# Layer 0 input of an MLA and Hyena trunk: adaLN weights loaded first, x divided by its rms ahead of adaLN, and the q projection moved among the filters with its result kept in DRAM

## The chip, the core and the metric

The kernel runs on one core of a Trainium2 chip. Matrix products run on TensorE (PE, whose weight loads the profile shows apart as PEld), elementwise work on VectorE (DVE) and ScalarE (ACT). Transfers are issued from two queues, that of SyncE (SP) and that of GpSimd (POOL), and carried out by the core's 16 DMA engines. The metric is the device time of one execution in microseconds (us), as the median of several runs; lower is better.

## What is computed

A trunk of two layers over 1024 latent tokens of width 1024, with 256 context tokens beside them. Layer 0 mixes tokens by multi-head latent attention (MLA), layer 1 by a Hyena long convolution. Each layer is x + gate * mixer(modulate(rmsnorm(x))), where shift, scale and gate come from a conditioning vector through adaLN. What matters here is the input side of layer 0, and the Hyena filters, which depend on weights alone and are worked out beside it. Cut from the reference, with the adaLN line and the line of the filters put in words:

```python
def rmsnorm(x, g):
    y = xf * lax.rsqrt(jnp.mean(xf * xf, axis=-1, keepdims=True) + NORM_EPS)
    return (y * g).astype(x.dtype)

def modulate(h, shift, scale):
    return h * (1 + scale) + shift
...
# adaLN: shift, scale, gate = split(silu(c) @ ada_w + ada_b)     a = modulate(rmsnorm(x, g), shift, scale)
cq, ckv, k_rope, gate = jnp.split(t @ w_in, splits, axis=-1)     # 384, 256, 64, 1024 columns
q = (rmsnorm(cq, q_norm_g) @ w_uq).reshape(B, n, MLA_HEADS, MLA_NOPE + MLA_ROPE)
kv = (rmsnorm(ckv, kv_norm_g) @ w_ukv).reshape(B, n, MLA_HEADS, MLA_NOPE + MLA_V)
...
# Hyena filters: an MLP over positions, times a decay, then transformed to the frequency domain
```

## The kernel before

Arrays lie transposed, features on the 128 partitions and tokens along the free axis, in tiles of 128x512 in fp32. A product whose operands carry more than one pass of TensorE keeps (`mm3`, L119 to L121) is made of three matmuls: each operand is split into a high and a low part (`split`: the ACT copy at L96 gives the high part, the DVE subtraction at L97 the low one), and high x high (L119), high x low (L120) and low x high (L121) are added in PSUM.

`layer0_in` (L446 to L626) covers everything up to attention. Its parts, by the names that the profile shows:

- **Weights.** `feed` and `weights` (L101 to L115) load pieces of the input projection (`wr`, 256 KB) and split them into `w`, two ahead of use. The list given to `feed` names the output blocks of 128 columns in their order of use: 0 to 7 are gates, 8 to 10 the latent kv and the rotary key, 11 to 13 the latent q.
- **adaLN** (`ada`, L147 to L177). For layer 0's shift and scale, 32 weight tiles `pg<-in_adaw` of 256 KB, four of them to each of eight groups of packed matmuls (`ad<-pg,sc`, L128). The rest of adaLN (32 tiles `aw<-in_adaw` of 512 KB in two buffers, groups `ad<-aw,sc`) is taken up beside the projections.
- **The rms** of x (`rms`, L360 to L393): squares on ACT, sums by packed matmuls with `ones` (L128), a transposition (L381) and a chain of small DVE instructions, L385 to L392, up to `rms`. `spread` (L395 to L401) broadcasts it over the partitions by transpositions into a PSUM tile R (L399).
- **`modulate`** (L403 to L408). For each tile x * gs * R on DVE (L406), the high part with the shift on ACT (L407), the low part on DVE (L408).
- **The filters** (`filters`, L271 to L361), a generator in eight groups g. In each, eight steps make `ph` (L318 and L319 on PE), multiply it by the decay `dec` (`kk`, L321 on DVE) and form sums and differences `kp` and `km` (L328, L329); then a transform (`rg`, `rt`, `blk`, L222 and L225 on DVE), the split of its blocks into `bh` and `bl`, and 75 matmuls `u<-bh,fm`, `u<-bl,fm` against transform tables `fm`, in blocks whose results `ko` are written to DRAM (`kd<-ko`, L351). The eight tables, 3.28 MB, come once, over POOL's queue (L295), after small POOL copies (L294) that wait for a tile given to the generator with `send`.
- **Projections** (`project`, `pj<-pg,w`). One output block is 48 matmuls of 128x512 over both token halves. `gates` passes it through SiLU and writes it to `gate_d` in DRAM. `latent_kv`, for x, and `context`, for the context tokens, norm their result (`normed`, L502 to L513, whose multiplication is L508), split it and write both parts to DRAM (`ckv_d`, `kr_d`). `latent_q` norms and splits directly into the SBUF tiles `cq` that attention reads.

The filters and the generator `work` (gates 0 to 5, `latent_kv`, `context`, the rest of adaLN) are interleaved: after every step of the filters, as many steps of `work` are taken as the ratio 60 to 120 allows (L604 to L609). When the filters are through, `attention_loads` (L629 to L651) loads kv and key back over POOL's queue (`ckv`, `krh`, `krl`), the attention weights are split, and meanwhile `latent_q` runs with gates 6 and 7 between its steps. The attention loop follows, whose first products are the keys (`pj<-ckv,wc`) and the queries (`pj<-cq,wb`, `pj<-cq,wa`).

Every engine runs its instructions in one fixed order that is written when the kernel is built. Buffers of the next stage are laid over those that the stage before releases, so that a load waits until their last reader or writer is done.

## Time and profile before

| | us |
|---|---|
| median of 3 runs | 1741.19 (1737.99 to 1742.52) |
| the profiled execution, its own time | 1735.72 |
| span of that execution in the profile | 1733.9 |
| first projection matmul of layer 0 | 78.09 |
| last filter matmul (`u`) | 407.34 |
| first product with the latent q | 440.91 |

The mean granted TensorE clock was 0.976 of full speed. In the rows of the profile, times count from the start of the span; a row of the timeline gives the start, the duration, engine, line, operation and tiles, and in brackets how long the engine was idle ahead of it and what released it. A row of instructions that follow one another is put together with its count (x8).

### The profile page before, as it was taken

What the parts mean: (1) busy time and instruction counts of PE and PEld (TensorE: products, weight loads), DVE (VectorE), ACT (ScalarE), POOL (GpSimd) and SP (SyncE); (2) the same over time, 40 slices, a digit from 0 to 9 for tenths busy, and PEclk for the clock granted to TensorE, in tenths of its full rate; (3) what the DMA queues carried; (4) which work ended last, traced back from release to release, by engine and by line L of the source; (5) the groups of instructions that cost most, each with busy time, mean ns of one, the idle gap of its engine ahead of it and who ended that gap; (6) DMA issues with size and microseconds to landing.
All of it is one profiled execution on the core that took longest, in us unless ns stands there. A gap on an engine that the chain in (4) does not pass through costs nothing.

```text
span 1733.9 us, 22766 instructions
## 1 busy us (share of the span) xinstructions
PE 1635.3 (94%) x8096; PEld 1300.2 (75%) x8096; DVE 1442.4 (83%) x2539; ACT 766.1 (44%) x1331; POOL 15.4 (1%) x43
## 2 busy tenths in 40 slices
PE   6799897898999999999999999999999999999995
PEld 2467676686788788788787777888888888887873
DVE  4885978895598899899889466999999999999856
ACT  4533444435455555455556345433433433433313
POOL 1000000000000000000000010000000000000000
PEclk8899998999999999999999999999999999999998
DMA  9777563436101001010013781332332332334555
GB/s 341 255 231 222 182 191 118 147 95 196 37 22 42 25 26 37 25 33 25 19 56 121 233 268 64 101 97 84 100 117 83 104 111 85 102 113 138 175 158 204
DMA packets 139030, 207.19 MB, mean 119 GB/s; under 512 B 13386, under 2 KB 67361, under 8 KB 138788
## 3 DMA queue, kind: packets, MB, share of 16 engines
q1 hardware_dynamic: 135780, 195.05, 35.7%
q0 software_dynamic: 3136, 10.69, 1.9%
q8 instruction: 64, 1.05, 0.2%
q14 instruction: 50, 0.41, 0.1%
HBM read 149.97 MB, written 53.61 MB: 117 GB/s over the span
## 4 chain that ended last, share of the span: by engine, by line
PE 79%; DMA 8%; DVE 8%; ACT 3%; issue 1%; SPq 1%; DVEq 0%; ACTq 0%
PE pj L121 13%; PE pj L119 13%; PE pj L120 12%; PE O L120 2%; PE S L119 2%; PE O L119 2%; PE S L811 2%; DMA kd<-ko 2%; PE O L121 2%; PE apx L747 2%; PE S L810 2%; PE S L121 2%; PE S L120 2%; PE apx L748 2%; DMA aw<-in_adaw 2%; PE fu L119 2%
## 5 line engine op out<-in xcount | busy, mean ns | idle before, releaser
L96 ACT CAST w<-wr 128x512 fp32r<-128x512 f32 (+1 forms) x154 | 93.7, 609 | 259.2 <-PE pj L120 134.3
L119 PE MATMUL pj<-a,w 128*128 128x512 f32 x512 | 203.3, 398 | 1.7 <-ACT a L407 1.6
L121 PE MATMUL pj<-a,w 128*128 128x512 f32 x512 | 203.3, 398 | 0.0
L120 PE MATMUL pj<-a,w 128*128 128x512 f32 x512 | 203.2, 397 | 0.0
L813 ACT ACTIVATE p<-S 128x512 f32<-128x512 f32 x160 | 95.5, 597 | 148.2 <-DVE acc L820 69.5
L97 DVE TENSOR_TENSOR w<-wr,w 128x512 fp32r<-128x512 f32 (+1 forms) x154 | 102.4, 673 | 56.5 <-ACT w L96 56.3
L96 ACT CAST bh<-raw 128x512 fp32r<-128x512 f32 x128 | 77.0, 620 | 88.8 <-DVE raw L1056 71.1
L119 PEld LDWEIGHTS pj<-a,w 128*128 128x128 f32 x512 | 96.5, 189 | 22.0 <-ACT a L407 2.4
L120 PEld LDWEIGHTS pj<-a,w 128*128 128x128 f32 x512 | 96.6, 189 | 19.8 <-DVE a L408 0.2
L121 PEld LDWEIGHTS pj<-a,w 128*128 128x128 f32 x512 | 96.7, 189 | 19.4 <-issue 0.8
L97 DVE TENSOR_TENSOR p<-p 128x512 fp32r<-128x512 f32 x160 | 109.5, 685 | 1.5 <-ACT p L96 1.2
L749 DVE TENSOR_REDUCE cm<-apx 128x1 f32<-128x512 f32 (+1 forms) x192 | 107.3, 592 | 3.8 <-PE apx L748 3.0
L121 PE MATMUL pj<-pg,w 128*128 128x512 f32 (+1 forms) x248 | 98.0, 395 | 9.5 <-DVE w L97 9.5
L820 DVE TENSOR_TENSOR acc<-acc,p 128x512 f32<-128x512 f32 x144 | 98.9, 687 | 7.6 <-ACT p L813 6.7
L96 ACT CAST p<-p 128x512 fp32r<-128x512 f32 x160 | 99.4, 622 | 4.8
L119 PE MATMUL pj<-pg,w 128*128 128x512 f32 (+1 forms) x248 | 96.7, 393 | 2.4 <-ACT pg L407 2.4
L120 PE MATMUL pj<-pg,w 128*128 128x512 f32 (+1 forms) x248 | 98.1, 396 | 0.6 <-DVE pg L408 0.6
L97 DVE TENSOR_TENSOR bl<-raw,bh 128x512 fp32r<-128x512 f32 x128 | 84.9, 688 | 9.1 <-ACT bh L96 8.9
L119 PE MATMUL u<-bh,fm 128*128 128x256 f32 (+1 forms) x200 | 67.8, 340 | 11.6 <-ACT bh L96 9.0
L321 DVE TENSOR_TENSOR kk<-ph,dec 128x512 f32<-128x512 f32 x64 | 42.9, 685 | 35.4 <-DMA dec<-in_dec 28.2
L747 PE MATMUL apx<-kn,qn 128*128 128x512 f32 (+1 forms) x192 | 69.1, 364 | 2.3 <-DVE cm L749 1.9
L748 PE MATMUL apx<-krh,r 128*128 128x512 f32 (+1 forms) x192 | 67.2, 358 | 0.0
(304 smaller groups left out, 4392.4 us busy)
## 6 DMA issues: line engine op xcount, KB each, us to landing
aw<-in_adaw SPq DMA_DIRECT2D x32, 512.0 KB
kd<-ko SPq DMA_DIRECT2D x128, 128.0 KB
wr<-in_hw SPq DMA_DIRECT2D x64, 256.0 KB
kt<-kd SPq DMA_DIRECT2D x56, 256.0 KB
wr<-in_w SPq DMA_DIRECT2D x34, 256.0 KB
dec<-in_dec SPq DMA_DIRECT2D x64, 128.0 KB
pg<-in_adaw SPq DMA_DIRECT2D x32, 256.0 KB
wr<-in_wo SPq DMA_DIRECT2D x32, 256.0 KB
```

The source lines that it names most:

```text
L96: self.nc.scalar.copy(out=hi, in_=raw)
L97: self.nc.vector.tensor_tensor(out=lo, in0=raw, in1=hi, op=ALU.subtract)
L119: mm(out, lhsT=w[0], rhs=x[0], start=start, stop=False)
L120: mm(out, lhsT=w[0], rhs=x[1], start=False, stop=False)
L121: mm(out, lhsT=w[1], rhs=x[0], start=False, stop=stop)
L321: nc.vector.tensor_tensor(out=kk, in0=ps, in1=dec.broadcast_to([P, 2, 2, P]), op=ALU.mult)
L747: mm(b[:, :w], lhsT=qn[0][:, c], rhs=kn[0][:, o : o + w], start=True, stop=False)
L748: mm(b[:, :w], lhsT=r1[:, c], rhs=krh[:, o : o + w], start=False, stop=True)
L749: v.tensor_reduce(out=cm[:, t, i : i + 1], in_=b[:, :w], axis=AX.X, op=ALU.max)
L810: mm(S, lhsT=krh[:, c], rhs=r1, start=False, stop=False)
L813: act.activation(out=p, in_=S, func=AF.Exp, scale=ASCALE)
L820: v.tensor_tensor(out=acc, in0=acc, in1=p, op=ALU.add)
```

## The change

The input of layer 0 is reordered and partly rewritten:

- `modulate` is replaced for layer 0 by two functions. `normalize` multiplies x by the spread rms in place (L415, DVE, one instruction for each tile). `shifted` then forms x * gs + shift twice, on ACT into the high part (L420) and on DVE in place (L421, TENSOR_SCALAR), and subtracts (L422, DVE). Layer 1 keeps `modulate`.
- The first half of x is normalised ahead of adaLN, its second half and the context later. The rms of the second half and of the context are worked out where they are used.
- The loop over adaLN's eight groups no longer steps the filters, so that nothing of them is asked for between the adaLN weights. The second half of x and the context are loaded behind these. The tables `fm` are released by the last tile of the second half of x (`x[1][7]`) rather than by that of the first.
- `latent_q` moves into `work`, behind `context`. Its result is written to DRAM (`cq_d`, six high and six low pieces of 256 KB) and loaded back by `attention_loads` with six loads of 512 KB on POOL's queue.
- Gates come in pairs, 0 and 1, 2 and 3, 4 and 5, and gates 6 and 7 last, behind the filters. The ratio of steps is now 66 to 128.

```diff
+    def normalize(self, xs, r, bank):
+        n = xs[0].shape[-1]
+        R = self.spread(r, n // P, bank)
+        for x in xs:
+            self.nc.vector.tensor_tensor(out=x, in0=x, in1=R[:, :n], op=ALU.mult)
+
+    def shifted(self, x, gs, sh, hi, lo):
+        nc = self.nc
+        nc.scalar.activation(out=hi, in_=x, func=AF.Identity, scale=gs, bias=sh)
+        nc.vector.tensor_scalar(out=x, in0=x, scalar1=gs, scalar2=sh, op0=ALU.mult, op1=ALU.add)
+        nc.vector.tensor_tensor(out=lo, in0=x, in1=hi, op=ALU.subtract)
...
+        self.cq_d = [self.dram.tile([KQ, P, L], F32, name=f"cq_d{r}") for r in range(2)]
...
-        self.feed([a["w1"][m] for m in (0, 1, 2, 8, 9, 10, 3, 4, 8, 9, 10, 5, 11, 12, 13, 6, 7)])
+        self.feed([a["w1"][m] for m in (0, 1, 8, 9, 10, 2, 3, 8, 9, 10, 11, 12, 13, 4, 5, 6, 7)])
...
         load_x(0)
-        rx = [self.rms(x[0], 512, bank, page)]
-        filt.send(x[0][7])
-        for n, _ in enumerate(self.ada([(0, 0, 4)], lambda n: page(), abank, 512)):
-            next(filt)
-            if n == 7:
-                load_x(1)
-                rx.append(self.rms(x[1], 512, bank, page))
+        self.normalize(x[0], self.rms(x[0], 512, bank, page), bank)
+        for _ in self.ada([(0, 0, 4)], lambda n: page(), abank, 512):
+            pass
+        load_x(1)
         load_c()
         xcs = [xc[k // 2][:, LC * (k % 2) : LC * (k % 2) + LC] for k in range(KD)]
-        rc = self.rms(xcs, LC, bank, page)
+        filt.send(x[1][7])
         ax = []
-        for xs, r in zip(x, rx):
-            R = self.spread(r, 4, bank)
+        for h, xs in enumerate(x):
+            if h:
+                self.normalize(xs, self.rms(xs, 512, bank, page), bank)
...
-                self.modulate(xs[k], R, gs[:, k, 0:1], res[:, k, 0:1], hi, lo)
+                self.shifted(xs[k], gs[:, k, 0:1], res[:, k, 0:1], hi, lo)
...
         def latent_q():
...
-            more = gates(range(6, 8))
             for h, sl in enumerate(halves):
-                for _ in normed([t[h] for t in ts], "qg", self.att[3], sl, True):
-                    next(more, None)
-                    yield
-            yield from more
+                yield from normed([t[h] for t in ts], "qg", self.cq_d, sl)
...
-            for _ in gates(range(0, 3)):
+            for _ in gates(range(0, 2)):
...
-            for _ in gates(range(3, 5)):
+            for _ in gates(range(2, 4)):
...
             yield from context()
-            for _ in gates(range(5, 6)):
+            yield from latent_q()
+            for _ in gates(range(4, 6)):
...
-            while n * 120 < (step + 1) * 60:
+            while n * 128 < (step + 1) * 66:
...
-        for _ in latent_q():
-            next(loads, None)
         for _ in loads:
             pass
+        for _ in gates(range(6, 8)):
+            pass
...
         nc.gpsimd.dma_start(out=krl, in_=self.kr_d[1])
         yield
+        for k in range(KQ):
+            for r in range(2):
+                nc.gpsimd.dma_start(out=cq[r][k], in_=self.cq_d[r][k])
```

What the change moves on PE ahead of the first projection. Before, filter matmuls `u` of the first group stand in front of `pj<-pg,w`; this is the end of that stretch:

```order
L119 MATMUL u<-bh,fm_103 128x256
L120 MATMUL u<-bl,fm_103 128x256
L121 MATMUL u<-bh,fm_104 128x256
L119 MATMUL u<-bh,fm_103 128x512
L120 MATMUL u<-bl,fm_103 128x512
L119 MATMUL pj<-pg,w 128x512
```

And now at the same place:

```order
L128 MATMUL ad<-aw,sc 32x512 x4
L128 MATMUL pj<-pg,ones 32x512 x4
L319 MATMUL ph<-fw,hr 128x256
L319 MATMUL ph<-fw,hf 128x256
L318 MATMUL ph<-fw,hr 128x256
L319 MATMUL ph<-fw,hr 128x256
L381 MATMUL pj<-ident,pg 128x128 x4
L128 MATMUL ad<-aw,sc 32x512 x4
L399 MATMUL pj<-ident,rms 128x128 x4
L119 MATMUL pj<-pg,w 128x512
```

No `u` stands ahead of the first projection any more (53 of them before, as counted over the whole order); five groups of the rest of adaLN (`ad<-aw,sc`, one before) and the sums, transposition and spread of the second half's rms do.

On SP's queue, before, from the first of the other adaLN weights (`aw`) to the second half of x, with the decay tiles `dec` between the adaLN weights:

```order
L156 DMA aw<-in_adaw 128x1024 x2
L156 DMA pg<-in_adaw 128x512 x8
L314 DMA dec<-in_dec 128x256
L156 DMA pg<-in_adaw 128x512 x4
L314 DMA dec<-in_dec 128x256
L156 DMA pg<-in_adaw 128x512 x4
L314 DMA dec<-in_dec 128x256
```

and now, at the same place:

```order
L156 DMA aw<-in_adaw 128x1024 x2
L156 DMA pg<-in_adaw 128x512 x32
L314 DMA dec<-in_dec 128x256 x2
L112 DMA wr<-in_w 128x512
L303 DMA fwr<-in_fwout 128x512
L112 DMA wr<-in_w 128x512
L481 DMA pg<-in_xT 128x512 x8
L485 DMA pg<-in_ctxT 128x512 x4
L156 DMA aw<-in_adaw 128x1024 x2
L314 DMA dec<-in_dec 128x256 x2
```

All 32 adaLN tiles stand back to back, and the last decay tiles of the first filter group stand behind x, the context and other adaLN weights.

On POOL's queue the loads for attention, before, were these seven:

```order
L641 DMA ckv_3997<-ckv_d_80 128x1280
L641 DMA ckv_3998<-ckv_d_80 128x1280
L641 DMA ckv_3999<-ckv_d_81 128x1280
L641 DMA ckv_4000<-ckv_d_81 128x1280
L646 DMA krh<-kr_d_82 64x1280 x2
L647 DMA krl<-kr_d_83 65x1280
```

and now, from the keys on (the four loads of `ckv` stand ahead of them as before):

```order
L654 DMA krh<-kr_d_84 64x1280 x2
L655 DMA krl<-kr_d_85 65x1280
L659 DMA cq_4332<-cq_d_82 128x1024
L659 DMA cq_4335<-cq_d_83 128x1024
L659 DMA cq_4333<-cq_d_82 128x1024
L659 DMA cq_4336<-cq_d_83 128x1024
L659 DMA cq_4334<-cq_d_82 128x1024
L659 DMA cq_4337<-cq_d_83 128x1024
```

Six loads of the latent q are new, last on the queue; the last of them (the third low piece) is first needed by the fifteenth matmul of the queries (before, by the eighth, since all of one weight's products stood ahead of the other's). Between the last `u` and the first query PE now has 37 projection matmuls and 18 of the keys; before it had 84 and 18, beside the norms of q.

More of the change, by code (lines that the diff above doesn't have):

```diff
@@ L500, in hilo_out, with normed @@
             nc.sync.dma_start(out=dsts[1], in_=lo.bitcast(F32)[:n])
-        def normed(xs, g, dst, sl, sbuf=False):
+        def normed(xs, g, dst, sl):
             n = sl.stop - sl.start
@@ L509, in normed @@
             for k, t in enumerate(xs):
-                if sbuf:
-                    self.split(t, dst[0][k][:, sl], dst[1][k][:, sl])
-                else:
-                    hilo_out(t, P, [d[k, :, sl] for d in dst])
+                hilo_out(t, P, [d[k, :, sl] for d in dst])
         def context():
-            R = self.spread(rc, 2, bank)
+            self.normalize(xcs, self.rms(xcs, LC, bank, page), bank)
+            yield
             ac = [[], []]
@@ L522, in context @@
                     sl = slice(LC * q, LC * q + LC)
-                    self.modulate(xcs[k + q], R[:, :LC], gs[:, k + q, 1:2], res[:, k + q, 1:2], hi[:, sl], lo[:, sl])
+                    self.shifted(xcs[k + q], gs[:, k + q, 1:2], res[:, k + q, 1:2], hi[:, sl], lo[:, sl])
                     ac[0].append(hi[:, sl])
```

## The prediction

> **What bounds the kernel now.** I read the page first, for the engine that sets the time, then the busy time by stretch, then PE's timeline in the stretches that the change touches.
>
> ```profile
> span 1733.9 us, 22766 instructions
> PE 1635.3 (94%) x8096; PEld 1300.2 (75%) x8096; DVE 1442.4 (83%) x2539; ACT 766.1 (44%) x1331; POOL 15.4 (1%) x43
> ```
>
> PE is busy for 94% of the span. A change in order can only gain where PE stands idle, and the change touches nothing behind the first queries of attention. So the question is how much PE idles up to there. The windows answer for it has, in each row, the stretch, its length, the busy time of the five engines, TensorE's clock, the DMA share and GB/s. The bounds are the first projection (78) and the last filter matmul with the start of the queries (407.5 and 440.9).
>
> ```profile
> 0.00:78.00 78.00, 52.99 (x252) 25.23 (x253) 47.76 (x112) 35.25 (x65) 5.76 (x20) 0.82 0.91 307
> 78.00:407.50 329.50, 296.68 (x1593) 234.94 (x1592) 270.46 (x558) 142.79 (x255) 0.00 (x0) 0.95 0.55 168
> 407.50:440.90 33.40, 27.75 (x122) 20.81 (x119) 13.46 (x25) 13.34 (x24) 3.69 (x7) 0.95 0.75 217
> ```
>
> PE idles 78.00 - 52.99 = 25.0 us in the start, where the DMA engines are busy for 0.91 of the time; 329.5 - 296.7 = 32.8 in the stretch of filters and projections, where DVE, at 270.5, is not far behind; and 33.4 - 27.75 = 5.7 in the tail. Those 63.5 us are all that can be had.
>
> **The change, part by part: the start.** PE's timeline shows what stood ahead of the first projection: adaLN's groups, waiting for weights, then the first filter matmul, then the first projection.
>
> ```profile
> 26.73 1.94 PE L128 MATMUL ad<-pg,sc 128*32 128x512 f32 x8
> 32.55 1.06 PE L128 MATMUL ad<-pg,sc 128*32 128x512 f32 x8 [1.90 <-DMA pg<-in_adaw]
> 52.34 1.94 PE L128 MATMUL ad<-pg,sc 128*32 128x512 f32 x8 [1.43 <-DMA pg<-in_adaw]
> 60.30 0.47 PE L119 MATMUL u<-bh,fm 128*128 128x512 f32 x1 [2.08 <-issue]
> 78.09 0.40 PE L119 MATMUL pj<-pg,w 128*128 128x512 f32 x1
> 79.73 1.07 PE L128 MATMUL ad<-aw,sc 128*32 128x512 f32 x8
> 85.77 1.07 PE L128 MATMUL ad<-aw,sc 128*32 128x512 f32 x8 [0.51 <-DMA aw<-in_adaw]
> 92.03 1.93 PE L128 MATMUL ad<-aw,sc 128*32 128x512 f32 x8 [1.47 <-DMA aw<-in_adaw]
> 101.15 1.06 PE L128 MATMUL ad<-aw,sc 128*32 128x512 f32 x8 [0.84 <-DMA aw<-in_adaw]
> ```
>
> adaLN now ends at 52.34 + 1.94 = 54.3. Its weights shared the DMA engines with the tables `fm`, which POOL issued as soon as the first half of x was there. The next rows are POOL's issue of them, and, from the DMA view of the first 60 us, the packets, MB and share of POOL's queue (q0) and the rate in 40 slices of 1.5 us.
>
> ```profile
> 13.68 4.39 POOL L295 DMA_DIRECT2D fm<-in_fm  x8
> q0 software_dynamic: 1152, 3.28, 15.2%
> GB/s 0 127 257 219 277 288 362 406 386 333 335 321 354 395 391 391 397 391 391 398 391 395 404 386 385 380 378 382 362 363 387 331 354 352 340 365 335 377 392 296
> ```
>
> Without the 3.28 MB of `fm` and the 128 KB decay tiles that stood between the weights, adaLN's last weight comes 3.28 / 0.39 = 8.4 us sooner for the tables, and some 4 to 5 for the rest: an estimate from these rows puts the last group at about 41, 13 us ahead. That is a gain only if the first projection follows. By the order it doesn't: between adaLN and the first projection PE now has five groups of the other adaLN weights instead of one. These come from two buffers and were 85.77 - 79.73 = 6.0 and 92.03 - 85.77 = 6.3 us apart. They stand on SP's queue behind the second half of x and the context (3.1 MB, 8 us at 391 GB/s). Five groups from about 41 + 8 on, 6 us apart, put the last at 49 + 4 x 6 = 73, beside the 3.28 MB of `fm`, which POOL now asks for at about 48 and which again run beside what PE waits for. On DVE, the second half's rms now stands behind the eighth product `kk`, whose decay tile comes behind those same weights, and behind the first transform. That transform took, before, from the end of this product to the first `u` at 60.30:
>
> ```profile
> 49.36 0.69 DVE L321 TENSOR_TENSOR kk<-ph,dec 128x512 f32<-128x512 f32 x1 [1.48 <-DMA dec<-in_dec]
> ```
>
> With that chain (11 us from the last `kk`, of which about half lies ahead of the rms) the first projection is possible at 72 to 84. I take 78, where it was: **0 us**, between -6 and +6.
>
> One rule of the Trainium skill speaks against loads on POOL's queue here. In the trace, the eight issues of `fm` took 4.39 us together, 0.55 each, with two instructions of the kind TENSOR_SCALAR on DVE in that time. The page "SBUF — State Buffer", in "SBUF: two separate sides", says that GpSimd can't write the descriptors of its transfers while a DVE instruction in a two-port mode holds the port pair that the two share. By that rule the eight new TENSOR_SCALAR (L421) of the first half, which run at about that time, would hold `fm` up by at most 8 x 0.44 = 3.5 us, by the durations below, and the sum would be 3.5 higher; the issues that the trace shows give no sign of such a delay, and I add nothing.
>
> **The stretch, PE.** Before, 84 projection matmuls of 128x512 stood behind the last `u`, those of q among them; now it is 37, of gates 6 and 7. The stretch gets the other 47. In a warm stretch one starts 435.25 - 435.02 = 0.23 us behind the other:
>
> ```profile
> 435.02 0.40 PE L121 MATMUL pj<-pg,w 128*128 128x512 f32 x1
> 435.25 0.39 PE L119 MATMUL pj<-pg,w 128*128 128x512 f32 x1
> 407.46 0.60 PE L399 MATMUL pj<-ident,rms 128*128 128x128 f32 x4
> 407.99 1.06 PE L128 MATMUL pj<-st,ones 128*32 128x512 f32 x6
> 410.01 0.50 PE L381 MATMUL pj<-ident,st 96*128 96x96 f32 x4
> 413.99 0.62 PE L399 MATMUL pj<-ident,rms 128*128 128x128 f32 x4 [0.48 <-DVE rms L392]
> ```
>
> That is 47 x 0.23 = 10.8, and the sums and spreads of q's norm, 0.60 + 1.06 + 0.50 + 0.62 = 2.8, come with it. The start gives up work as well: 53 of the first group's 75 matmuls `u` were done before 78.09 (14 of 512 columns at 0.23, 39 of 256 at half of it: 7.7) and the context's rms (about 1.5); none is done there now, while four more groups of `ad` (1.07 each, 4.3) are: +4.9. In all 10.8 + 2.8 + 4.9 = **18.5** of PE work more.
>
> **The stretch, DVE.** The rows by form, with count, sum and mean duration:
>
> ```profile
> L408 DVE SCALAR_TENSOR_TENSOR pg<-pg,adac 128x512 fp32r<-128x512 f32 x16 | 11.9, 745 | 3.6 <-ACT pg L407 3.6
> L406 DVE SCALAR_TENSOR_TENSOR pg<-pg,gs,pj 128x512 f32<-128x512 f32 x16 | 11.8, 741 | 0.0
> L508 DVE SCALAR_TENSOR_TENSOR pg<-pg,cols,pj 128x512 f32<-128x512 f32 x10 | 7.0, 744 | 4.1 <-PE pj L399 4.1
> L97 DVE TENSOR_TENSOR cq<-pg,cq 128x512 fp32r<-128x512 f32 x6 | 3.9, 686 | 6.4 <-DMA kd<-ko 6.4
> L205 DVE TENSOR_SCALAR nrnd<-arg 128x512 f32<-128x512 f32 x6 | 2.6, 439 | 10.4 <-ACT arg L203 10.3
> ```
>
> A tile of x took 0.74 + 0.75 = 1.49; it now takes 0.69 (L415) + 0.44 (L421, as L205; 0.69 if it were no cheaper than the others) + 0.69 (L422) = 1.82, so 16 tiles cost 16 x 0.33 = 5.3 more (9.3 at most), and the context's eight half tiles about 1.5. Six tiles of q bring 6 x 0.70 + 3.9 = 8.1. Even with none of it in the start that is +15: 285 of DVE work beside 296.7 + 18.5 = 315 of PE's. PE bounds the stretch, and the edits on DVE cost nothing by themselves; the cover is PE's work, and without it they would cost those 15.
>
> How much of the 18.5 shows? The stretch's idle time of 32.8 comes in short waits for DVE, ACT and the transform, spread over eight filter groups, and the orders of the engines are fixed. I let all but the waits for `aw` stay: 0.51 + 1.47 + 0.84 = 2.8 of these move into the start with their groups. So the last `u` comes 18.5 - 2.8 = **15.7 us later**, between -2.8 (all the added work falls into idle time) and 18.5 + 5.5. The 5.5 are what a norm in the midst of the filters can bring in new waits, as the one of kv did before:
>
> ```profile
> 201.57 0.46 PE L381 MATMUL pj<-ident,st 64*128 64x64 f32 x4 [1.14 <-ACT st L378]
> 203.82 0.36 PE L318 MATMUL ph<-fw,hf 128*128 128x256 f32 x1 [1.12 <-DVE rms L389]
> 207.81 0.55 PE L318 MATMUL ph<-fw,hf 128*128 128x256 f32 x1 [3.28 <-DVE rms L392]
> ```
>
> The twelve writes to `cq_d` (3.1 MB) go over SP's queue in a stretch at 168 GB/s of the 390 seen above: hidden.
>
> **The tail.** From the last `u` to the eighth query matmul it took 35.3 us before, nearly all of it work; its one large wait is that of 4.76, and behind it 7 matmuls ran at half pace:
>
> ```profile
> 407.34 0.28 PE L121 MATMUL u<-bh,fm 128*128 128x256 f32 x1
> 429.93 0.79 PE L121 MATMUL pj<-pg,w 128*128 128x512 f32 x1 [4.76 <-DVE w L97]
> 433.08 0.48 PE L119 MATMUL pj<-pg,w 128*128 128x512 f32 x1
> 442.64 0.39 PE L120 MATMUL pj<-cq,wb 128*128 128x512 f32 x1
> 407.80 0.53 POOL L641 DMA_DIRECT2D ckv<-ckv_d  x1 [389.73 <-PE u L121]
> 425.46 0.69 DVE L97 TENSOR_TENSOR cq<-pg,cq 128x512 fp32r<-128x512 f32 x1 [6.38 <-DMA kd<-ko]
> ckv<-ckv_d POOLq DMA_DIRECT2D x4, 640.0 KB, 7.5
> krl<-kr_d POOLq DMA_DIRECT2D x1, 325.0 KB, 13.7
> ```
>
> PE now has 37 projections (8.5), the keys (3.4) and 14 queries (3.2) before it needs the last piece of q: 15 us of work. But q comes by DMA, and the loads stand on POOL's queue behind the seven that began, at 407.80, only when the last `u` had let `fm`'s memory go. The last piece lies where before the last low piece of q lay, whose writer waited until 425.46, 17.8 us behind the last `u`, for the filters' last writes `kd<-ko`. With a landing of 7.5 (13.7 for the slower ones) q is whole 17.8 + 7.5, about 26 us behind the last `u`, between 22 and 31. At that point 14 queries are done, where before 7 were done at 35.3: a gain of 35.3 - 26 + 7 x 0.23 = 10.9, less 1.5 for a second slow restart behind a wait of 11 (as from 429.93 to 433.08: 7 steps of 0.43 instead of 0.23, 1.4). **-9.4 us**, between -13.4 and -4.4.
>
> **The sum.** 0 + 15.7 - 9.4 = +6.3, against the profiled execution 1735.7 + 6.3 = 1742.0. That execution lies 5.5 below the median of the three runs (1741.19), so the forecast is 1747.5, rounded to 1748. A measurement of this kernel can tell about 0.3%, 5.2 us, from no change.
>
> **The rivals.**
> Faster (on the other side): the work that is moved fills PE's idle time in the stretch. For it: PE has 32.8 us of it there and the added 18.5 would fit; DVE at 285 of 329 also would. Against it: the orders are fixed, and PE is busy for 0.90 of the stretch already. If all fits, the stretch is 2.8 shorter, the sum 0 - 2.8 - 9.4 = -12.2, the time 1729. It decides from the point where the stretch grows by less than 9.4 - 5.2 = 4.2.
> No change: the first projection profits by about half of adaLN's 13 us, 6.3, since its waits for `aw` and for the transform overlap. For it: the transfers of the start run at 0.91 and the bytes ahead of the first projection are the same less some `dec`. Against it: the five groups. The sum is about 0, the time 1741.
> Slower still: q comes at 31 and its norms bring waits like those of kv: 6.3 + 5.0 + 5.5 = 16.8, the time 1758; with the start 6 late 1764.
> That the change doesn't do what it says is no case: the order shows all parts of it.
>
> **How the numbers follow.** The forecast has 0.35, slower still 0.12, no change 0.24, faster 0.29. So slower by over 0.3% has 0.35 + 0.12 = 0.47, the same 0.24, faster 0.29. The range runs from the full price of the faster case, 1728, to that of the slower one with its start, 1765; the forecast's own, with the bounds of the tail and half of those of the start, is 1740 to 1756.
>
> **What would show it.** The last group of `ad<-pg,sc` ends near 41 and the first projection stands near 78. From there to the last `u` the stretch is near 345 with PE idle for about 30: if the idle time has fallen under 20, the faster case is right. Behind the last `u`, PE waits once for some 11 us, at a query matmul, for `cq<-cq_d`, at about 26 us. The forecast is wrong if the first projection is before 72, if that wait is under 5 us, or if the stretch is within 5 us of what it was.

## The result and the profile after

The changed kernel takes 1763.37 us (median of 4 runs) where the kernel before takes 1741.86 (4 runs): a ratio of 1.0133, with a 95% interval of 1.0106 to 1.0160. It is slower, as forecast, but by 23 us where the forecast had 6.

The profiled execution of the changed kernel took 1763.63, beside a span of 1761.8. The head of its page:

```profile
span 1761.8 us, 22823 instructions
PE 1641.2 (93%) x8096; PEld 1302.0 (74%) x8096; DVE 1447.9 (82%) x2563; ACT 764.2 (43%) x1329; POOL 20.9 (1%) x49
```

The same three stretches by windows (length, busy time of PE, PEld, DVE, ACT and POOL, clock, DMA share, GB/s): up to the first projection, up to the last `u`, up to the last query matmul.

```profile
0.00:85.00 85.00, 47.27 (x208) 18.16 (x209) 48.06 (x106) 31.36 (x52) 6.93 (x20) 0.76 0.88 308
85.00:441.70 356.70, 317.25 (x1702) 253.45 (x1701) 285.29 (x608) 151.68 (x278) 0.00 (x0) 0.94 0.52 158
441.70:469.80 28.10, 20.58 (x75) 14.30 (x73) 4.28 (x6) 6.66 (x13) 6.92 (x13) 0.90 1.09 341
```

The start is 6.9 us longer (85.0 for 78.1), the stretch 27.2 (356.7 for 329.5), and the tail, up to the last query matmul, 9.6 shorter (from 441.56 to 469.53 for 407.34 to 444.90). That is 24.6 at the end of the queries; another 3.3 lie in the unchanged rest, which in the profiled executions of all the kernels here took between 1289 (before) and 1299 (`start_only`) by itself. The profiled execution of before lay below its median, so the medians are 21.5 apart where the profiles are 27.9 apart.

PE's timeline of the start, after: the last of adaLN's groups, the five groups of the other adaLN weights, the second half's sums, the first projection.

```profile
41.85 1.94 PE L128 MATMUL ad<-pg,sc 128*32 128x512 f32 x8 [1.58 <-DMA pg<-in_adaw]
46.73 1.60 PE L128 MATMUL ad<-aw,sc 128*32 128x512 f32 x8
55.73 1.94 PE L128 MATMUL ad<-aw,sc 128*32 128x512 f32 x8 [7.40 <-DMA aw<-in_adaw]
68.42 1.93 PE L128 MATMUL ad<-aw,sc 128*32 128x512 f32 x8 [7.52 <-DMA aw<-in_adaw]
75.31 1.93 PE L128 MATMUL ad<-aw,sc 128*32 128x512 f32 x8 [2.46 <-DMA aw<-in_adaw]
77.02 1.81 PE L128 MATMUL pj<-pg,ones 128*32 128x512 f32 x8
82.34 1.94 PE L128 MATMUL ad<-aw,sc 128*32 128x512 f32 x8 [2.14 <-DMA aw<-in_adaw]
85.01 0.67 PE L119 MATMUL pj<-pg,w 128*128 128x512 f32 x1
```

adaLN ends at 43.8, 10.5 us sooner than before, and the first projection comes 6.9 us later.

PE's waits in the stretch, after (85 to 441.7): what waits, for what, us in all, times, the longest.

```profile
PE u L119 <- ACT bh L96: 12.8, 7, 8.4
PE ad L128 <- DMA aw<-in_adaw: 12.6, 5, 5.0
PE ph L318 <- DVE kk L321: 3.7, 4, 1.7
PE ph L318 <- DVE rms L388: 2.9, 2, 1.5
PE ph L318 <- DVE rms L386: 2.7, 1, 2.7
```

And the same of before (78 to 407.5):

```profile
PE u L119 <- ACT bh L96: 9.0, 5, 6.4
PE ad L128 <- DMA aw<-in_adaw: 8.0, 7, 1.7
PE pj L121 <- DVE w L97: 4.8, 3, 3.4
PE ph L318 <- DVE rms L392: 3.3, 1, 3.3
```

The waits for `aw` were to fall from 8.0 to 5.2; they are 12.6, with three fewer groups in the stretch.

The tail, after: two keys and the query that uses q's last piece, on PE; the issue of that piece on POOL.

```profile
441.56 0.28 PE L121 MATMUL u<-bh,fm 128*128 128x256 f32 x1
453.90 0.69 PE L120 MATMUL pj<-ckv,wc 128*128 128x512 f32 x1 [1.55 <-DMA ckv<-ckv_d]
468.08 0.80 PE L120 MATMUL pj<-cq,wb 128*128 128x512 f32 x1 [1.92 <-DMA cq<-cq_d]
458.41 0.53 POOL L659 DMA_DIRECT2D cq<-cq_d  x1 [3.74 <-ACT kn L96]
```

q's last piece is issued 16.9 us behind the last `u` and used 26.5 us behind it. The 1.92 are PE's longest wait for q; all its waits for q and kv together are 6.9 us.

### The profile page after: what moved, and what is told of

Its sections match the earlier page's. It is cut to its first block, busy times and chain, and to the rows that moved or that the text cites. A ratio compares the mean times of both kernels' runs of the same rounds, so it can differ in the third digit from the quotient of the medians.

```text
span 1761.8 us, 22823 instructions
## 1 busy us (share of the span) xinstructions
PE 1641.2 (93%) x8096; PEld 1302.0 (74%) x8096; DVE 1447.9 (82%) x2563; ACT 764.2 (43%) x1329; POOL 20.9 (1%) x49
## 5 line engine op out<-in xcount | busy, mean ns | idle before, releaser
L97 DVE TENSOR_TENSOR w<-wr,w 128x512 fp32r<-128x512 f32 (+1 forms) x154 | 102.4, 672 | 54.2 <-ACT w L96 54.1
L97 DVE TENSOR_TENSOR p<-p 128x512 fp32r<-128x512 f32 x160 | 109.4, 684 | 1.6 <-ACT p L96 1.3
L120 PE MATMUL pj<-pg,w 128*128 128x512 f32 (+1 forms) x248 | 96.3, 388 | 0.8 <-DVE pg L422 0.7
L119 PE MATMUL pj<-pg,w 128*128 128x512 f32 (+1 forms) x248 | 96.4, 389 | 0.0
L121 PE MATMUL pj<-pg,w 128*128 128x512 f32 (+1 forms) x248 | 95.4, 385 | 0.0
L97 DVE TENSOR_TENSOR bl<-raw,bh 128x512 fp32r<-128x512 f32 x128 | 84.8, 686 | 9.1 <-ACT bh L96 8.8
```

The lines of the kernel that those rows point to most:

```text
L97: self.nc.vector.tensor_tensor(out=lo, in0=raw, in1=hi, op=ALU.subtract)
L119: mm(out, lhsT=w[0], rhs=x[0], start=start, stop=False)
L120: mm(out, lhsT=w[0], rhs=x[1], start=False, stop=False)
L121: mm(out, lhsT=w[1], rhs=x[0], start=False, stop=stop)
```

## The experiments

Each kernel was timed beside the kernel before on the same chip, and stands here by its ratio to that, with the interval; 0.0010 is 1.7 us. Kernels are compared by their ratios; a difference given with ± takes the intervals of both into account. One profile of a kernel is one execution, which can lie several us from the median of its runs.

**First: the two halves of the change, and the waits for `aw`.** After the profile the first theory (W) was that the loss is these waits.

`start_only` is the changed kernel with everything of the moved q undone:

```diff
-            yield from latent_q()
...
-            while n * 128 < (step + 1) * 66:
+            while n * 120 < (step + 1) * 60:
...
+        for _ in latent_q():
+            next(loads, None)
```

> The new start alone: load order, normalize and shifted, no filter steps during adaLN, tables released by the second half of x. The q projection, the order of the gates and the ratio of steps are those of the kernel before. Theory W (the groups of the other adaLN weights, which the new start draws ahead of and among the projections, each wait for a transfer: 32.1 us of waits in the changed kernel's PE rows against 8.0 before): 14 to 22 us slower than before, first projection near 85. Theory Q (the loss is that of moving the q projection into the filters): within 5 us of before.

1.0045 (1.0021 to 1.0068), 8 us slower than before; first projection at 83.5. More than theory Q and less than W. Its profile doesn't show where the time goes: the last query stands at 447.4, 2.5 later than before's 444.9, and the other 10 of the 12.6 us between the two spans lie in the rest behind it, which the change doesn't touch.

`q_only` is the kernel before, with the moved q alone (and the new list in `feed`, the new pairs of gates, the new ratio of steps and the loads on POOL's queue):

```diff
+            yield from latent_q()
...
-                for _ in normed([t[h] for t in ts], "qg", self.att[3], sl, True):
-                    next(more, None)
-                    yield
+                yield from normed([t[h] for t in ts], "qg", self.cq_d, sl)
```

> The start of the kernel before, with the q projection moved, its result kept in DRAM, and the new order of gates and ratio of steps. Theory W: between 6 us faster and 4 us slower than before, first projection near 78. Theory Q: 12 to 22 us slower than before.

1.0026 (1.0005 to 1.0048), 4.5 slower. The two halves alone cost 8 + 4.5, and together 23: there is an interaction of some 11 us (± 7).

`aw_after` holds the groups of the other adaLN weights back:

```diff
+            with self.tc.issue_after(after.ins):
+                prev = mm(*mms[-1], len(mms) - 1)
...
-                         for q, w in enumerate(cols)])
+                         for q, w in enumerate(cols)], self.last if width > 512 else None)
```

> The changed kernel, with each group of the other adaLN weights held in PE's order behind the last projection matmul that the program had written before it; nothing is left out. Theory W: none of these groups stands ahead of the first projection, which comes at 65 to 73, PE's waits for aw fall under 8 us in all, and the time is 17 to 28 us below the changed kernel's. Theory Q: less than 7 us below it.

1.0165 (1.0125 to 1.0206): not faster at all, and W fails as it was put. PE's waits for `aw` fall from 32.1 us in all to 16.7 rather than under 8, all of them now behind the first projection, and other waits take the place of the rest. PE's timeline of its start:

```profile
55.66 0.58 PE L322 MATMUL ph<-fw,hf 128*128 128x256 f32 x1 [8.28 <-DVE kk L325]
65.98 0.58 PE L322 MATMUL ph<-fw,hf 128*128 128x256 f32 x1 [2.14 <-DVE kk L325]
79.80 0.78 PE L119 MATMUL pj<-pg,w 128*128 128x512 f32 x1
```

With the five groups gone from there, PE waits in the same place for `kk`, whose decay tiles stand late on SP's queue, and the first projection comes 5.2 us sooner.

`fm_early` gives the tables back their place:

```diff
         load_x(0)
+        filt.send(x[0][7])
...
-        filt.send(x[1][7])
```

> The changed kernel with the transform tables released by the first half of x, as before the change. If the tables' sharing of the DMA engines is what makes the groups of the other adaLN weights late (theory F): first projection near 77 and 7 to 12 us below the changed kernel. If the round trip of two buffers is, whatever runs beside it (theory W in its narrow form): within 4 us of the changed kernel, since adaLN's own weights then come some 8 us later.

1.0182 (1.0142 to 1.0222), first projection at 89.9: theory F fails, and moving the tables back gains nothing. The groups of the other adaLN weights do come closer, 9.5, 8.1, 7.2 and 6.0 us apart where they were 9.0, 12.7, 6.9 and 7.0, but adaLN itself now ends at 54.1, 10 us later.

**Second: where in the stretch.** The first `u` of each filter group, the projections that stand ahead of it in PE's order, and the ends of the stretches give this table (us; number of projection matmuls):

| | to the first `u` of the second filter group | from there to the last `u` | from there to the last query |
|---|---|---|---|
| before | 128.8 (128) | 278.5 (532) | 37.6 (84) |
| q_only | 130.9 (142) | 282.8 (529) | 32.5 (73) |
| changed | 148.1 (192) | 293.4 (515) | 28.0 (37) |

A matmul is 0.23 us. Against `q_only`, which moves q as well, the changed kernel is 17.2 us later in the first part with 50 matmuls (11.5) more done, 10.6 longer in the second with 14 (3.2) fewer, and 4.6 shorter in the third with 36 (8.3) fewer. So it loses 5.7, 13.8 and 3.7. The middle part by filter group, changed kernel (windows, the columns as above):

```profile
190.00:251.70 61.70, 48.47 (x276) 32.23 (x274) 39.55 (x88) 21.95 (x41) 0.00 (x0) 0.90 0.71 226
251.70:295.80 44.10, 30.80 (x195) 26.02 (x191) 37.17 (x88) 20.35 (x40) 0.00 (x0) 0.89 0.46 134
341.10:390.40 49.30, 41.84 (x219) 33.83 (x219) 41.20 (x93) 23.23 (x43) 0.00 (x0) 0.93 0.50 156
```

In the first row PE idles 13.2 us. All eight groups of the second set of adaLN weights lie there, each a transfer of 1 MB into the same two buffers, one round trip after the other:

```profile
235.14 1.54 PE L128 MATMUL ad<-aw,sc 128*32 128x512 f32 x8 [0.55 <-DMA aw<-in_adaw]
242.94 1.94 PE L128 MATMUL ad<-aw,sc 128*32 128x512 f32 x8 [3.94 <-DMA aw<-in_adaw]
249.84 1.94 PE L128 MATMUL ad<-aw,sc 128*32 128x512 f32 x8 [4.96 <-DMA aw<-in_adaw]
```

The second row holds the context, the third the norm of q. DVE is busy for longer than PE in the second and for as long in the third, and PE idles 13.3 and 7.5. The context is no part of the loss, though: its filter group in the kernel before was as long and idled 12.6.

```profile
269.40:313.50 44.10, 31.49 (x184) 27.41 (x184) 39.54 (x83) 18.92 (x39) 0.00 (x0) 0.85 0.41 119
```

The other filter groups of before's middle part idle between 0 and 6.1. What grew is the idle time of the first row and of the third. Over the whole middle part, by windows between the same two points (us):

| | length | PE busy | PE idle |
|---|---|---|---|
| before | 278.5 | 249.9 | 28.7 |
| q_only | 282.8 | 248.4 | 34.4 |
| changed | 293.4 | 254.4 | 39.0 |
| aw_spread | 286.8 | 253.0 | 33.8 |
| q_nonorm | 284.6 | 246.4 | 38.2 |
| spread_nonorm | 279.6 | 247.2 | 32.4 |

The last three rows are of kernels that follow.

`aw_spread` spreads those eight groups:

```diff
-            for _ in gates(range(2, 4)):
-                next(gen, None)
+            for i, _ in enumerate(gates(range(2, 4))):
+                if i % 2 == 0:
+                    next(gen, None)
                 yield
...
-            yield from latent_q()
+            for i, _ in enumerate(latent_q()):
+                if i % 3 == 0:
+                    next(gen, None)
+                yield
```

> The changed kernel, with the second set of eight adaLN groups (layer 0's gate and layer 1's) spread by the program over gates 2 and 3 and the q projection, so that five and three of them fall into two filter groups where all eight fell into one. Theory L (lumps: the eight in one filter group waited 12.1 us for their transfers, with no projections left to cover them): 5 to 11 us below the changed kernel, waits for aw in the stretch under 7. Rival (PE then waits as long for something else in the same filter groups): within 3 us of it.

1.0098 (1.0070 to 1.0126), 6 us below the changed kernel (± 7), as L has it. The times alone leave it open; the profile bears it out. The waits of its stretch (84.2 to 435.4):

```profile
PE u L119 <- ACT bh L96: 13.2, 6, 8.7
PE ad L128 <- DMA aw<-in_adaw: 6.0, 3, 4.1
PE ph L318 <- DVE rms L386: 2.7, 1, 2.7
```

The waits for `aw` are halved, and the middle part is 286.8 for 293.4, 5.2 of the difference being idle time. The filter group that held all eight groups of `ad` is 50.0 long instead of 61.7, with five of them:

```profile
190.90:240.90 50.00, 43.56 (x252) 30.90 (x251) 37.95 (x83) 21.89 (x41) 0.00 (x0) 0.96 0.72 216
```

`steps_back` steps the filters during adaLN again:

```diff
         for _ in self.ada([(0, 0, 4)], lambda n: page(), abank, 512):
-            pass
+            next(filt)
```

with the tables released by the first half of x, as in `fm_early`, here behind its multiplication.

> The changed kernel, with the filters stepped again during adaLN and the tables released by the first half of x; normalize and shifted, the late load of the second half of x, the late rms and the moved q stay. Theory S (the start's loss, 11.6 us more of PE's time without work up to the first projection, comes of the filter steps that are no longer there to fill adaLN's waits, and the distribution of the projections that follows from it costs the rest): 13 to 24 us below the changed kernel, first projection 76 to 82. Theory X (it comes of the later load and rms of the second half of x): less than 6 below, first projection still at 83 or later.

1.0082 (1.0053 to 1.0110), 9 below the changed kernel: between S and X. Its first projection is at 99.7, with the first group's `u` ahead of it again. The early multiplication of x now stands in front of the filters' products on DVE, and with them SP's queue; its rows on DVE and SP:

```profile
30.34 4.87 DVE L415 TENSOR_TENSOR pg<-pg,pj 128x512 f32<-128x512 f32 x8 [1.26 <-PE pj L399]
48.27 0.69 DVE L321 TENSOR_TENSOR kk<-ph,dec 128x512 f32<-128x512 f32 x1 [7.53 <-DMA dec<-in_dec]
36.36 0.33 SPq L314 DMA_DIRECT2D dec<-in_dec  x1
36.73 1.92 SPq L156 DMA_DIRECT2D pg<-in_adaw  x4
```

The decay tile at 36.36 waits for its buffer, which the product behind L415 has to release, and the adaLN weights wait behind the tile.

`q_nonorm` leaves out the norm of the latent q:

```diff
+            if g == "qg":
+                yield
+                for k, t in enumerate(xs):
+                    hilo_out(t, P, [d[k, :, sl] for d in dst])
+                return
```

> The changed kernel without the norm of the latent q: its rms, the spread and the six multiplications (L508) are left out, and the projection is split and written as it is. Theory N (the norm makes its filter group wait for DVE: 12.8 us lost between the sixth and the seventh group, with waits for rms of 5): 6 to 11 us below the changed kernel. Rival (the group is bound by DVE's other work): 1 to 4 us below.

1.0103 (1.0051 to 1.0155), 5 below (± 10): between N and its rival, and with an interval that reaches both. In the profile the middle part is 284.6 for 293.4, but 8.0 of these 8.8 us are time in which PE was busy, and the idle time is nearly the same. In the filter group that holds q (337.3 to 379.3) the waits for `rms` are gone, and PE still idles 6.1 us, 3.7 of them for a split of weights on DVE (`w`, L97). So the gain is work left out rather than waits, and the profile speaks for the rival: without the norm DVE has 35.3 us of other work in this group of 42.0.

`pace54` draws less work among the filters:

```diff
-            while n * 128 < (step + 1) * 66:
+            while n * 128 < (step + 1) * 54:
```

> The changed kernel with the ratio of steps 54 to 128 instead of 66 to 128, so that 192 projection matmuls are left for the last filter group and the tail where 45 were. Theory P (the ratio draws too much work ahead of the last u and leaves the tail without cover for q's loads): 8 to 15 us below the changed kernel. Theory L: 2 to 6 below, by the spread of the adaLN groups (three and five) alone.

1.0179 (1.0139 to 1.0219), 8 us above the changed kernel (± 8): P fails, and L's sum with it. Two of its filter groups, with 15 and 38 projection matmuls in them, show why:

```profile
148.00:184.00 36.00, 26.41 (x146) 20.04 (x147) 32.95 (x73) 16.78 (x30) 0.00 (x0) 0.87 0.49 143
368.40:404.90 36.50, 26.02 (x151) 21.11 (x151) 31.62 (x65) 14.77 (x27) 0.00 (x0) 0.93 0.38 112
```

A filter group takes 36 us here with little else for PE to do, and 32 to 33 of them are DVE's. In the kernel before a group with 84 projections took 34. So work taken out of a group leaves PE idle.

**Third: the parts of the new start, and the two lumps together.**

`arith_only` is the kernel before with the new arithmetic in the old places (for the context too):

```diff
             R = self.spread(r, 4, bank)
+            for k in range(KD):
+                v.tensor_tensor(out=xs[k], in0=xs[k], in1=R, op=ALU.mult)
...
-                self.modulate(xs[k], R, gs[:, k, 0:1], res[:, k, 0:1], hi, lo)
+                self.shifted(xs[k], gs[:, k, 0:1], res[:, k, 0:1], hi, lo)
```

> The kernel before, with modulate replaced by the multiplication with the spread rms and shifted for x and the context, in the same places; order of loads, filters and q as before. The forecast costed these edits at nothing beside PE's work (theory C): within 4 us of before. Theory D (DVE sets several filter groups, so that its 7 us more of work show): 4 to 8 us slower, most of it in the first filter group, where the multiplications fall.

1.0009 (0.9991 to 1.0026), 1.6 us: by the times C holds in the old order. The profiled execution was the slowest of this kernel's ten, 5.9 above their median, and it has the loss where D puts it: the first `u` of the second filter group at 136.9 for 128.8, and the last query at 452.2 for 444.9. PE's waits ahead of that `u` (60 to 137) are 9.6 for `aw` where before had 3.5. So D is not excluded.

`order_only` is `start_only` with `modulate` back, that is the new order of loads and steps alone (the context is changed in the same way, with one step fewer):

```diff
-        self.normalize(x[0], self.rms(x[0], 512, bank, page), bank)
+        r = self.rms(x[0], 512, bank, page)
...
-                self.normalize(xs, self.rms(xs, 512, bank, page), bank)
+                r = self.rms(xs, 512, bank, page)
+            R = self.spread(r, 4, bank)
...
-                self.shifted(xs[k], gs[:, k, 0:1], res[:, k, 0:1], hi, lo)
+                self.modulate(xs[k], R, gs[:, k, 0:1], res[:, k, 0:1], hi, lo)
```

> The new start with the arithmetic of before: no filter steps during adaLN, the second half of x, the context and the tables loaded behind adaLN, each half's rms where it is used, modulate as before; q, gates and ratio as before. Theory S (the order of loads and steps costs the start's loss): 5 to 10 us slower than before, as the whole new start (8.2), first projection near 80. Theory D: within 4 us of before.

0.9983 (0.9960 to 1.0006): S fails, the new order by itself costs nothing that can be told. Its first projection:

```profile
59.63 1.47 PE L128 MATMUL pj<-pg,ones 128*32 128x512 f32 x8
67.99 1.94 PE L128 MATMUL ad<-aw,sc 128*32 128x512 f32 x8 [5.52 <-DMA aw<-in_adaw]
74.74 0.78 PE L119 MATMUL pj<-pg,w 128*128 128x512 f32 x1
```

The last of the second half's sums stand at 59.6, behind two groups of `ad` (in the changed kernel at 77.0, behind four), and the first projection at 74.7. So under the new order the new arithmetic costs 1.0045 - 0.9983, 11 us (± 6); in the profiles the last query stands at 436.2 here and at 447.4 in `start_only`.

`before_lump` holds the second set of adaLN groups back in the kernel before:

```diff
-            for _ in gates(range(0, 3)):
-                next(gen, None)
+            for i, _ in enumerate(gates(range(0, 3))):
+                if i < 8:
+                    next(gen, None)
```

> The kernel before, with the second set of eight adaLN groups held back by the program to the steps of gates 3 and 4, so that six of them fall into the fourth filter group where two to four fell into each. Theory L (a lump of such groups in one filter group waits for transfers that nothing covers): 3 to 8 us slower than before, waits for aw 12 or more in the stretch (8.0 before). Rival: within 2 us of before.

0.9983 (0.9959 to 1.0006), with waits for `aw` of 9.8 in the stretch: L fails here, and the middle part idles 28.3 us where before idled 28.7. A lump doesn't cost by itself; this one has six groups for eight and 86 projections beside it for 79, and what else lets it pass was not taken apart.

`spread_nonorm` is `aw_spread` and `q_nonorm` in one.

> The changed kernel with the second set of adaLN groups spread, and without the norm of the latent q (its rms, spread and six multiplications are left out). If the two are separate parts of what the moved q costs under the new start (theory L with theory N): 11 to 15 us below the changed kernel, that is 7 to 12 above before, as the new start alone. Rival (either one takes the same time away, since another wait comes in its place): 6 to 9 below the changed kernel.

1.0057 (1.0040 to 1.0075), 13 us below the changed kernel and 10 above before, as expected of two separate parts. Its middle part is 279.6 for 293.4. Of these 13.8 us 7.2 are PE's busy time, mostly the work that is left out, and 6.6 idle time. That the first table also has 13.8 lost there is chance, since it compares with `q_only`, which has the norm as well.

**Fourth: the arithmetic with q moved, and the tail.**

`q_order` is the changed kernel with the edit of `order_only`; `q_order_spread` has that of `aw_spread` as well; `late_norm` is `start_only` with the first half multiplied behind adaLN:

```diff
-        self.normalize(x[0], self.rms(x[0], 512, bank, page), bank)
+        r = self.rms(x[0], 512, bank, page)
...
-            if h:
-                self.normalize(xs, self.rms(xs, 512, bank, page), bank)
+            self.normalize(xs, self.rms(xs, 512, bank, page) if h else r, bank)
```

> The changed kernel with modulate in place of normalize and shifted, all else as changed: the new order of loads and steps and the moved q without the new arithmetic. Theory A (under the new order of loads the arithmetic costs 11 us, since the chain of the second half's rms then stands behind five adaLN groups instead of three; with order_only against start_only): 9 to 13 us below the changed kernel, first projection near 75. Rival (the 11 us come only where q is not moved, and the changed kernel is held elsewhere): within 4 us of the changed kernel.

1.0106 (1.0073 to 1.0140), 5 below the changed kernel (± 7), first projection at 76.4. Less than theory A has, more than its rival; neither is settled by it.

> The kernel of q_order with the second set of adaLN groups spread over gates 2 and 3 and the q projection. If the arithmetic, the lump of adaLN groups (5.4 us as measured) and the moved q's norm (about 7) are separate and sum up: 15 to 19 us below the changed kernel, 4 to 8 above before. Rival: no further gain on q_order.

1.0082 (1.0052 to 1.0112), 9 below the changed kernel and 14 above before: the parts don't sum to the whole.

> The kernel of start_only with the first half of x multiplied by its rms behind adaLN, where modulate stood, instead of ahead of it; its five adaLN groups ahead of the first projection stay. Theory A (the price is that of the place of the first projection in PE's order, not that of the early multiplication): as start_only, 5 to 12 us slower than before, first projection near 84. Rival (the multiplication ahead of adaLN holds up the filters' products on DVE): within 4 us of before.

1.0046 (1.0020 to 1.0072), first projection at 85.3, as `start_only`, and five groups of `ad` ahead of it as there (three in `order_only`). So the early multiplication isn't what costs. That the place of the first projection is, as A has it, goes with the orders, but no kernel has the new arithmetic in the order of `order_only`.

`q_by_sp` puts q's loads on the other queue:

```diff
-                nc.gpsimd.dma_start(out=cq[r][k], in_=self.cq_d[r][k])
+                nc.sync.dma_start(out=cq[r][k].bitcast(F32), in_=self.cq_d[r][k])
```

> The changed kernel with the six loads of the latent q on SP's queue instead of POOL's; nothing else moves. Theory K (q is late because its memory waits for the filters' last writes, 17 us behind the last u, whichever queue asks): within 3 us of the changed kernel, last piece used 25 to 27 us behind the last u. Theory R (q is late because it stands on POOL's queue behind the seven loads of kv and key, whose issues wait for one another): 3 to 6 us below it, last piece used by 21 us behind the last u.

1.0118 (1.0077 to 1.0158), 2.6 below (± 8), within what K allows; the times can't tell K from R, but the profile can. The last piece is used 24.7 us behind the last `u` (at 442.8):

```profile
467.49 0.80 PE L120 MATMUL pj<-cq,wb 128*128 128x512 f32 x1 [0.48 <-DMA cq<-cq_d]
```

SP's queue waits 5.9 us in all for the filters' writes `kd<-ko` among q's six loads. In the changed kernel POOL's waits there end with landings of `ckv` and, for the last piece, with a copy on ACT.

`q_late` has the latent q behind gates 4 and 5, in the program of `q_order_spread` and in the list of `feed`:

```diff
-            for i, _ in enumerate(latent_q()):
-                if i % 3 == 0:
-                    next(gen, None)
-                yield
             for _ in gates(range(4, 6)):
                 next(gen, None)
                 yield
+            yield from latent_q()
```

> The kernel of q_order_spread with the latent q behind gates 4 and 5 instead of ahead of them. Theory N (q's norm brings more DVE work than its filter group has room for, whichever group it is): within 4 us of q_order_spread. Rival (in the last filter groups it lies beside the least DVE work): 5 to 10 us below it, near before.

1.0066 (1.0047 to 1.0085), 3 us below `q_order_spread`, as N has it. The difference is uncertain by ± 6, so that the rival's gain isn't excluded.

No version beat the kernel before by more than its interval; `order_only` and `before_lump` come nearest.

## Why the prediction was right in sign and short in size

**The start: "I take 78, where it was: 0 us".** The chain was right, adaLN ending near 41 (43.8) and the first projection waiting behind five groups. The spacing was wrong. The five groups were put 6 us apart, as in the stretch before; they came 9.0, 12.7, 6.9 and 7.0 apart. A group's load waits for its buffers, stands behind decay tiles on SP's queue, and shares the DMA engines with `fm`; with `fm` earlier (`fm_early`) the four distances were 4.8 us less in all, and how the rest divides was not taken apart. The first projection is at 85.0, one past the range that was given. By `aw_after` the groups are about half of the difference: with them moved, PE waited for the products of the decay tiles instead, and the first projection came at 79.8. `order_only` has it at 74.7: with `modulate`, the last of the second half's sums start 17 us earlier (59.6 for 77.0), behind two of these groups instead of four, under the same order of loads.

**"The edits on DVE cost nothing by themselves."** In the old order they cost 1.6 us by the times (`arith_only`, not to be told from none, though its one profile is 7 us later at the last query); in the new one it is 11 us between `order_only` and `start_only`. There PE's order changes with them, and this is the likely way in which they cost, but it was not tried by itself. With q moved as well they cost 5, less clearly.

**The stretch: "I let all but the waits for `aw` stay ... 15.7 us later."** This is the term that failed: it measured 27.2. The added work was about right (PE busy 20.6 more, 18.5 forecast), and so was its sum over the stretch (PE 317, DVE 285, where 315 and 285 were forecast). The step that failed is the idle time: 39.4 us where 32.8 - 2.8 = 30.0 were forecast, on the ground that PE bounds the stretch as a whole and that all waits but those for `aw` stay as they were. By filter group PE doesn't bound it. The shortest groups take 34 to 36 us, 31 to 33 of them DVE's, and work that falls together in one group waits there.

Two filter groups show it. The one with eight adaLN groups idles 13.2 us, 12.1 of them for `aw`; spread over two filter groups (`aw_spread`), the waits for `aw` are halved and the middle part idles 5.2 us less. The one with the moved q idles 7.5 us, most of it for the chain of its norm; without the norm (`q_nonorm`) it still idles 6.1, so that the norm's waits alone aren't the reason. The bound that the text gave for a norm's new waits, 5.5, is near the 5.7 us that PE waits for this chain there. The lump of adaLN groups was not thought of, since those of before were spread over three filter groups; and that a lump need not cost, `before_lump` shows.

**The tail: "-9.4 us".** It measured -9.6, and q's last piece came at 26.5 us where 26 was forecast. So the bound, q's arrival, was right. What PE does up to then was not: the text names a wait under 5 us at a query matmul as a sign of being wrong, and the longest was 1.92. The one wait of 11 came as 7.5 in all (28.10 less 20.58 of PE's work), spread over keys and queries, and the work up to the last query took 20.6 at a granted clock of 0.90, where some 16 were put down. That q's lateness is not POOL's queue was tried (`q_by_sp`). That it is the memory was not tried by itself, and the amount to be moved is a third explanation: the 16 DMA engines moved 341 GB/s in this stretch, at a share of 1.09, where the prediction's rows reach 406.

**The Trainium skill's rule.** The forecast added nothing for the rule that the Trainium skill gives in "SBUF — State Buffer", "SBUF: two separate sides", by which two-port DVE instructions hold up POOL's descriptors. The eight issues of `fm` took 4.40 us, as before (4.39), so the trace shows no such delay; but only one of the new TENSOR_SCALAR began during these issues, so it is hardly a test:

```profile
52.41 4.40 POOL L295 DMA_DIRECT2D fm<-in_fm  x8
56.76 0.54 DVE L421 TENSOR_SCALAR pg<-pg,gs,adac 128x512 f32<-128x512 f32 x1
```

**The rivals.** The faster one needed the added work to fill PE's idle time; that time grew instead. The slower one, with the start 6 us late, gave 1764, and 1763 was measured, but by luck: of its parts the late start came (6.9), while q did not come at 31 us (26.5) and the tail gained as forecast. The stretch made up for it, in part by the lump that no rival has.

**What stays open.** New order of loads and moved q cost 18 together (`q_order`), and -3 and 4.5 alone. The lump accounts for 4 to 6 of the 17 between (`q_order_spread`, `aw_spread`). Leaving out q's norm gains some 5 to 7 more, but mostly by work that `q_only` has as well, so it says little about this interaction; the larger part of it was not taken apart. Nor is it shown where the new start alone loses its 8 us.

## What to carry to other kernels

Where two streams of work are interleaved by hand, make the sum for each stage of the inner loop, not over the whole: an engine that is second over 357 us (DVE, 285 us to PE's 317) can be busy for longer than the first in some of the stages, and work moved into a stage without room shows. Loads into a single pair of buffers wait for one another: here eight groups in a row came 6 to 10 us apart and PE waited 12 us for them. Whether a step's place in the program spreads them is seen in the order, not in the diff. Costing an arithmetic edit by its instructions leaves out what the schedule makes of it; here the same edit cost 1.6 us (-1.6 to 4.5) in one order of loads and 11 (± 6) in another.

## What the runs showed of the hardware

A TENSOR_SCALAR on DVE with two scalars read from columns, written over its input, took longer than one of the same shape with two constants, written to another tile, whose row stands in the prediction (L205). The new one, as a group by form of the changed kernel:

```profile
L421 DVE TENSOR_SCALAR pg<-pg,gs,adac 128x512 f32<-128x512 f32 x16 | 8.7, 545 | 0.0
```

That is 545 ns beside 439; which of the two differences does it was not tried. So a tile of x costs 0.68 + 0.545 + 0.685 = 1.91 where 1.82 was forecast, 1.4 us more over 16 tiles.
